# Starting VectorE's background work one k-pass earlier, with shorter pauses, and moving one conditioning step ahead of a weight split

## The chip, the cores and the metric

The kernel runs on one core of one Trainium2 chip. The metric is the device time of one execution in microseconds (us); times of before and after are medians of several executions on the same kind of chip. A core has a matrix engine (TensorE, PE in the profile, with its weight loads as PEld), VectorE (DVE), ScalarE (ACT), GpSimd (POOL) and SyncE (SP). SP issues most of the transfers from main memory; POOL and ACT issue a few of their own. Each engine works through its own list of instructions in the order in which the program wrote them, so an instruction that waits holds up everything behind it on that engine.

## The reference, cut to what matters

One layer of a decoder for 256 tokens of width 2048, batch 1:

```python
mod = (silu(c) @ w_cond + b_cond).reshape(B, 3, 3, 2048)
u = x * (1 + mod[:, 0, 1]) + mod[:, 0, 0]
h = (silu(u @ w1) * (u @ w3)) @ w2                    # SwiGLU, hidden width 5632
x = layer_norm(ALPHA * x + 0.5 * (1 + mod[:, 0, 2]) * h)
...                                                   # mixer, modulated by mod[:, 1]:
proj = u @ w_in                                       # q, k, v and s
h = concat([diff_attention(q, k, v), s5_branch(s)], -1) @ w_out
x = layer_norm(ALPHA * x + (1 + mod[:, 1, 2]) * h)
...                                                   # second SwiGLU, modulated by mod[:, 2]
```

The S5 branch is a diagonal complex state-space model with 64 groups and 64 states. Its step matrices and decay tables depend on parameters alone, so they can be prepared at any time before the mixer needs them. The same holds for `mod`, which depends on `c` alone.

## The kernel before, in words

**Jobs.** The heavy work is a list of jobs. A job takes one 128x1024 piece of fp32 weights. SP loads it (`raw`), ScalarE casts it to a reduced format (`hi`, L690), VectorE subtracts to get what the cast lost (`lo`, in `pay`, L697), and TensorE multiplies with `hi` and `lo` against activations that are split into two parts in the same way (`Uh`/`Ul`, later `Hh`/`Hl` and so on). `Stream.run` (L703) writes the jobs in order: the hooks of a job, its matmuls, the split of the piece that comes `AHEAD` = 4 jobs later (2 in the first four jobs), then the background hooks `bg`, then `drain`. There are four buffers of `raw`, of `hi` and of `lo`. Nearly all VectorE and TensorE instructions pass a helper that adds up a cost estimate of each engine, so they have line 105 in the profile and are told apart by their tiles.

**The first feed-forward.** Its first 96 jobs (4 * `NT1`) are four k-outer passes of 24 jobs, each over four of the sixteen 128-row slices of the input. A pass can only start once its quarter of the input is modulated by `mod`. Sums that must be kept between passes lie in tiles `kosum`; in the later passes VectorE adds to them. 168 further jobs finish the hidden activations and do the down projection. The last four jobs do token half 0 first, then (in `last_block`) run its residual and layer norm on VectorE and ScalarE while TensorE does token half 1; then the first transposes of the mixer follow (`turn`).

**Conditioning.** `mod` is a matrix-vector product done by VectorE: `gv_step` (L230) multiplies one 128x1024 half row block of `w_cond` by silu(c) and accumulates along the row (tiles `early` for a whole 128x2048 block that counts as two steps, `gv` for a half). There are 288 steps. Sixteen of them complete one quarter of one modulation; `finish` (L256) then forms scale and shift of two or four slices and `modulate` queues the ScalarE work for them, which `pay_mod` and `pay_late` write out (ScalarE `uf` and `Uh`, VectorE `Ul`). Until step 64 the steps are tied to job numbers (`ahead`, L1534). Each step also asks SP for later rows of `w_cond` (`gv_load`).

**Background work.** After job 96 the rest of conditioning and the preparation of the S5 branch fill VectorE's gaps. `drain` (L360), called after every job, hands out work while VectorE's estimate is below that of TensorE plus `lim`. A credit of `gv_max` steps per job limits conditioning; the rising target `gv_due` says when conditioning has precedence over the S5 list `bg5`. The S5 list is `fill` (some 110 small operations on a tile `cells`), then `rest`: for each of four quarters a load, VectorE products, ScalarE copies, transposes on TensorE and stores, and at the end two halves of decay tables (`tables`, L595; tiles `tabc` and `tabr`, stored to `scrB` by POOL). Between them stand pauses, `wait(n)`; a pause ends when TensorE's estimate has moved on by n * `S5_WAIT`. What is left of the list three jobs before the end of the first feed-forward is written out at once by `drain_s5` (L380).

**The start.** Conditioning steps 0 to 7 give the first two input slices, steps 8 to 15 the next two. Jobs 0 to 3 use the first two slices, jobs 4 to 7 the next two. Steps 8 and 9 are tied to job 0, 10 and 11 to job 1, 12 and 13 to job 2, 14 and 15 to job 3; in each job the split of a weight piece stands ahead of the steps.

## Time and profile before

| what | value |
|---|---|
| median of 3 runs | 1934.16 us (1934.05 to 1934.27) |
| the profiled execution | 1936.67 us, of which the span from the first to the last instruction is 1934.9 us |
| mean granted TensorE clock | 0.982 of full |
| TensorE busy | 1861.1 us, 96% of the span |
| VectorE busy | 1490.3 us, 77% |
| ScalarE busy | 889.4 us, 46% |
| moved by DMA | 532.36 MB, 275 GB/s on average |

The table is read from the top of the profile's page. TensorE is the busiest by far, so what counts is the time in which it stands still, and the engine that it then waits for. The other engines' idle time costs nothing by itself. Timeline rows in the quoted fences give start and duration in us, engine, line, operation, the tile written, an arrow, the tiles read with shapes, and in brackets the idle time before the instruction and what ended it. Rows of a stretch ("stages") give start:end, length, then busy time with the count of instructions in parentheses for each engine shown, then the granted clock, the DMA share and GB/s.

### The profile page before, as it was taken

How to read it: one execution, taken by the hardware profiler on the slowest of the kernel's cores; microseconds unless marked ns; L12 is line 12 of the kernel's file. 1: busy time of each engine (PE TensorE's matmuls, PEld its weight loads, DVE VectorE, ACT ScalarE, POOL GpSimd, SP SyncE). 2: the span in 40 equal slices, each digit the busy share in tenths (PEclk: the TensorE clock that was granted, in tenths of full speed). 3: DMA queues.
4: the chain of work that ended last, by engine and by line, in shares of the span. 5: the costliest groups of instructions: out<-in, count | busy, mean ns of one | idle time of the engine just before them, and what ended most of it. 6: DMA issues, size and time to landing. Idle time of an engine off the chain costs nothing.

```text
span 1934.9 us, 25434 instructions
## 1 busy us (share of the span) xinstructions
PE 1861.1 (96%) x9326; PEld 1571.3 (81%) x9326; DVE 1490.3 (77%) x2255; ACT 889.4 (46%) x1211; POOL 64.0 (3%) x119
## 2 busy tenths in 40 slices
PE   5999999999999999589999998999999999999996
PEld 4888888888888887489998886888888888888885
DVE  5889878987887899887988997887875545454568
ACT  3554444445445543343447634544444444334442
POOL 0000000000000000202120000000000000000000
PEclk9999999999999999799999998999999999999998
DMA  8998857989999997698988885998888555565563
GB/s 329 374 346 311 300 177 246 318 279 357 313 339 346 319 349 272 215 349 272 310 272 297 288 321 199 332 355 292 286 281 270 190 187 185 196 216 186 192 231 110
DMA packets 151935, 532.36 MB, mean 275 GB/s; under 512 B 21841, under 2 KB 23297, under 8 KB 150657
## 3 DMA queue, kind: packets, MB, share of 16 engines
q1 hardware_dynamic: 137234, 495.32, 73.4%
q0 software_dynamic: 6512, 23.89, 3.6%
q10 hardware_dynamic: 8064, 11.54, 1.6%
q8 instruction: 73, 1.20, 0.2%
q14 instruction: 52, 0.43, 0.1%
HBM read 513.34 MB, written 17.33 MB: 274 GB/s over the span
## 4 chain that ended last, share of the span: by engine, by line
PE 83%; DMA 5%; DVE 5%; issue 5%; ACT 1%; POOL 0%; SPq 0%; ACTq 0%; DVEq 0%; POOLq 0%
PE ps L105 83%; DMA raw<-in_f1w_dram 2%; DMA early<-in_w_cond_dram 1%; DVE lo L105 1%; DVE Y L105 1%; DVE gv L105 1%; DVE early L105 1%; ACT hi L690 0%; DMA U<-sD 0%; DMA sD<-sT 0%; DVE tabc L105 0%; DMA s5e<-scrA 0%; DMA scrB<-tabr 0%; DMA raw<-in_f2w_dram 0%; ACT Y L861 0%
## 5 line engine op out<-in xcount | busy, mean ns | idle before, releaser
L105 DVE TENSOR_TENSOR lo<-raw,hi 128x1024 fp32r<-128x1024 f32 x630 | 766.5, 1222 | 351.7 <-ACT hi L690 343.3
L690 ACT CAST hi<-raw 128x1024 fp32r<-128x1024 f32 x630 | 661.5, 1053 | 702.5 <-PE ps L105 523.6
L105 PE MATMUL ps<-hi,Uh 128*128 128x512 f32 x1472 | 583.1, 396 | 19.3 <-ACT Uh L317 15.6
L105 PE MATMUL ps<-hi,Ul 128*128 128x512 f32 x1472 | 576.8, 392 | 0.0
L105 PE MATMUL ps<-lo,Uh 128*128 128x512 f32 x1472 | 456.5, 391 | 1.4 <-DVE lo L105 1.4
L105 PEld LDWEIGHTS ps<-hi,Uh 128*128 128x128 f32 x1472 | 278.3, 189 | 80.2 <-ACT Uh L317 16.5
L105 PEld LDWEIGHTS ps<-lo,Uh 128*128 128x128 f32 x1472 | 277.9, 189 | 61.1 <-DVE lo L105 2.6
L105 PEld LDWEIGHTS ps<-hi,Ul 128*128 128x128 f32 x1472 | 278.4, 189 | 56.6 <-DVE Ul L105 0.9
L105 DVE SCALAR_TENSOR_TENSOR gv<-gv,sc 128x1024 f32<-128x1024 f32 x258 | 314.1, 1218 | 2.3 <-DMA gv<-in_w_cond_dram 1.9
L105 PE MATMUL ps<-hi,Hh 128*128 128x512 f32 (+1 forms) x716 | 274.5, 385 | 0.0
L105 PE MATMUL ps<-hi,Hl 128*128 128x512 f32 (+1 forms) x716 | 273.6, 383 | 0.0
L105 PE MATMUL ps<-lo,Hh 128*128 128x512 f32 (+1 forms) x716 | 216.6, 384 | 3.5 <-DVE lo L105 3.5
L105 PEld LDWEIGHTS ps<-lo,Hh 128*128 128x128 f32 x716 | 133.0, 188 | 30.7 <-DVE lo L105 4.3
L105 PEld LDWEIGHTS ps<-hi,Hh 128*128 128x128 f32 x716 | 134.5, 188 | 26.6 <-issue 0.4
L105 PEld LDWEIGHTS ps<-hi,Hl 128*128 128x128 f32 x716 | 134.6, 188 | 26.1
L105 PE MATMUL ps<-Uh,hi 128*128 128x256 f32 x384 | 99.8, 296 | 2.4 <-ACT sT L1143 1.9
L105 PE MATMUL ps<-Ul,hi 128*128 128x256 f32 x384 | 97.4, 290 | 0.0
L105 PEld LDWEIGHTS ps<-Uh,hi 128*128 128x128 f32 x384 | 75.8, 197 | 6.5 <-ACT sT L1143 2.7
L105 PEld LDWEIGHTS ps<-Ul,hi 128*128 128x128 f32 x384 | 75.6, 197 | 0.6 <-DVE Ul L105 0.3
L1006 ACT CAST Hh<-ps 128x512 fp32r<-128x512 f32 x44 | 25.9, 588 | 75.0 <-PE ps L105 74.9
L105 DVE TENSOR_TENSOR Hl<-ps,Hh 128x512 fp32r<-128x512 f32 x44 | 30.3, 688 | 35.5 <-ACT Hh L1006 35.5
L105 PE MATMUL ps<-Uh,lo 128*128 128x256 f32 x384 | 53.9, 283 | 0.0
(229 smaller groups left out, 1398.4 us busy)
## 6 DMA issues: line engine op xcount, KB each, us to landing
raw<-in_f1w_dram SPq DMA_DIRECT2D x264, 512.0 KB, 5.8
raw<-in_f2w_dram SPq DMA_DIRECT2D x264, 512.0 KB, 4.8
gv<-in_w_cond_dram SPq DMA_DIRECT2D x258, 512.0 KB, 6.9
raw<-in_win_a_dram SPq DMA_DIRECT2D x48, 512.0 KB, 5.2
raw<-in_wout_dram SPq DMA_DIRECT2D x32, 512.0 KB, 5.8
early<-in_w_cond_dram SPq DMA_DIRECT2D x28, 512.0 KB, 7.7
s5m<-scrB POOLq DMA_DIRECT2D x8, 1024.0 KB, 9.2
raw<-in_win_v_dram SPq DMA_DIRECT2D x16, 512.0 KB, 5.2
```

The source lines that it names most:

```text
L105: return f(*a, **k)
L690: S.copy(hi, raw)
L1006: S.copy(hh, p)
```

## The change

Five edits. First, `drain` gets its limits at job `BG_AT` = 70 instead of 96, so that conditioning and the S5 list's `fill` may run in the last k-outer pass; `rest` still joins the list at job 96. The target `gv_due` starts at job 70 and has the same end (step 160 at job 256). Second, the limit of the first feed-forward goes from 2.6 to 3.0 and its credit from 0.62 to 0.57 steps per job. Third, the pauses: `S5_WAIT` goes from 2.0 to 1.7 and the pause between the two halves of the tables from 8.0 to 4.0. Fourth, steps 14 and 15 go from job 3 to job 2, and in job 2 the steps stand ahead of the split of the fifth weight piece. Fifth, the second weight piece is split ahead of the first modulation rather than behind it.

```diff
-LIM = (2.6, 100.0, 100.0, 100.0)
-GVM = (0.62, 0.65, 0.85, 0.4)
+LIM = (3.0, 100.0, 100.0, 100.0)
+GVM = (0.57, 0.65, 0.85, 0.4)
-S5_WAIT = 2.0
+S5_WAIT = 1.7
+BG_AT = 70
...
-            rest += [(0.0, tables(0)), wait(8.0), (0.0, tables(1))]
+            rest += [(0.0, tables(0)), wait(4.0), (0.0, tables(1))]
...
                     if not j.hold:
-                        self.split_to(self.done + st["split"])
+                        if self.done != 3:
+                            self.split_to(self.done + st["split"])
                         for f in j.bg:
                             f()
+                        if self.done == 3:
+                            self.split_to(self.done + st["split"])
                         drain()
...
+        stream.split_to(2)
         pay_mod()
-        stream.split_to(2, False)
         pay_late()
-        stream.pay()
...
-            n = (8 + 2 * i + 2 if i < 4 else NS + math.ceil((i - 3) * NS / (GA[0] - 3)) if i <= GA[0] else
+            n = ((10, 12, 16, 16)[i] if i < 4 else NS + math.ceil((i - 3) * NS / (GA[0] - 3)) if i <= GA[0] else
...
-        stream.run(4 * NT1)
+        stream.run(BG_AT)
         bg5.extend(fill)
-        bg5.extend(rest)
-        new_stats()
-
         n0 = stream.done
         st["gv_due"] = lambda n: 64 + 96.0 * (n - n0) / (GV_END - n0)
         st["lim"], st["gv_max"] = LIM[0], GVM[0]
+        stream.run(4 * NT1 - BG_AT)
+        bg5.extend(rest)
+        new_stats()
```

## The prediction, made before the run

> **What bounds the kernel now.** I read the head of the page first, then what TensorE waited for, then the timeline at each long wait.

> ```profile
> PE 1861.1 (96%) x9326; PEld 1571.3 (81%) x9326; DVE 1490.3 (77%) x2255; ACT 889.4 (46%) x1211; POOL 64.0 (3%) x119
> ...
> PE ps L105 <- ACT Y L861: 18.3, 1, 18.3
> PE ps L105 <- ACT Uh L317: 15.6, 2, 7.8
> PE ps L105 <- DVE Y L105: 6.3, 2, 3.3
> PE ps L105 <- DVE lo L105: 4.9, 3, 2.2
> ```

> TensorE is the bound; of its 1934.9 - 1861.1 = 73.8 us at rest, two items stand out: one wait of 18.3 us for the normalised `Y`, and two of 7.8 us for the modulated input `Uh`, one of them before the first job, which the change leaves. The first item is the end of the first feed-forward:

> ```profile
> 771.15 1.28 DVE L105 SCALAR_TENSOR_TENSOR Y<-X,Y 128x512 f32<-128x512 f32 x2
> 772.35 3.48 DVE L105 TENSOR_TENSOR lo<-raw,hi 128x1024 fp32r<-128x1024 f32 x3
> 775.75 0.41 DVE L105 TENSOR_TENSOR tabc<-tabc,tabr 128x256 f32<-128x256 f32 x1
> ...
> 783.12 0.07 DVE L105 MEMSET tabc<- 128x16 f32 x1 [3.23 <-DMA scrB<-tabc]
> 784.80 0.07 DVE L105 MEMSET tabc<- 128x16 f32 x1 [1.61 <-DMA scrB<-tabc]
> 786.24 0.69 DVE L105 COPY tabr<-cells 128x1024 f32<-128x1024 f32 x1 [1.36 <-DMA scrB<-tabr]
> ...
> 796.34 0.68 DVE L105 TENSOR_TENSOR r<-ps,G 128x512 f32<-128x512 f32 x1
> ...
> 782.46 0.40 PE L105 MATMUL ps<-lo,Hh 128*128 128x256 f32 x2
> 801.11 1.12 PE L105 MATMUL ps<-ident,Y 128*128 128x128 f32 x4 [18.25 <-ACT Y L861]
> ...
> 807.16 0.58 PE L105 MATMUL ps<-Uh,hi 128*128 128x256 f32 x1 [0.56 <-DVE Uh L105]
> ```

> The name ACT hides the cause. From 775.75 to 796.34 VectorE works through what was left of the S5 list: the last steps of the first table half, a wait of 3.23 + 1.61 + 1.36 = 6.2 us until that half is stored, then the whole second half. The residual `r` of the last block stands behind it, and the layer norm and the transposes behind that. The same place at the mixer's end, where no list is left, shows the clean case:

> ```profile
> 1171.88 0.40 PE L105 MATMUL ps<-lo,Ah 128*128 128x256 f32 x2
> 1172.12 0.60 PE L105 MATMUL ps<-ident,Y 128*128 128x128 f32 x4
> 1175.78 1.12 PE L105 MATMUL ps<-ident,Y 128*128 128x128 f32 x4 [3.06 <-DVE Y L105]
> 1177.45 0.80 PE L105 MATMUL ps<-hi,Uh 128*128 128x512 f32 x1 [0.56 <-DVE Uh L105]
> ```

> There the first token half is normalised under the matmuls of the second, and only a 3.06 us wait for the second half remains.

> **The tail of the first feed-forward.** From the last tail matmuls to the first of the next stage it takes 807.16 - 782.46 = 24.7 us here and 1177.45 - 1171.88 = 5.6 us there. If the list is empty in time, 24.7 - 5.6 = 19.1 us go. What is late next is the second half's `Y`, which I leave in the sum.

> Is the list empty in time? What has to move is 796.34 - 775.75 = 20.6 us of VectorE time, 14.4 without the waits for the store.

> ```profile
> 226.00:297.00 71.00, 52.60 (x65) 1.00 0.55 189
> 297.00:450.00 153.00, 136.02 (x289) 1.00 0.85 291
> 450.00:691.00 241.00, 195.93 (x290) 1.00 0.94 337
> 691.00:771.00 80.00, 77.28 (x144) 1.00 0.88 313
> ...
> 300.00:381.00 81.00, 19.20 (x113) 1.00 0.86 296
> ...
> L105 DVE SCALAR_TENSOR_TENSOR gv<-gv,sc 128x1024 f32<-128x1024 f32 x13 | 15.8, 1218 | 0.0
> ```

> The first four rows are VectorE's busy time by stretch, the fifth that of the operations on `cells`, nearly all of them `fill`, the sixth the conditioning steps from 691 to 771. The last pass (226 to 297) leaves 71 - 52.6 = 18.4 us free and holds no background work. From job 70 on the target asks for 96 / 186 = 0.516 steps per job, so 26 jobs take 13.4 steps of 1.218 us, 16.3 us, and some 2 us remain for `fill`; later the steps need 0.6 - 0.516 = 0.084 fewer per job, which over 165 jobs frees 16.9 us for the list. So whichever goes first, about 18 us of work move out of the later stretch. Then the pauses: their weights in the list add up to 73, at 2.0 this is 146 us of TensorE's estimate, and 69 at 1.7 is 117, 29 us less. They bind, since from 450 to 691 VectorE is idle for 241 - 195.9 = 45 us while the list is unfinished; from 691 on it has 2.7 us in 80 and the list crawls. Ending some 29 us of pauses and 18 us of work sooner covers 20.6 us, and the tables then run where there is idle time. I take the list as done. What hides it is VectorE's idle time under TensorE; if that cover is short, the price is the remaining VectorE time, one for one.

> The waits added: none by name, but shorter pauses can let VectorE, ScalarE or TensorE meet data not yet there. After the copies of a batch the pause ends after 6.8 us rather than 8, with the next weight split four jobs ahead; I cost it at nothing; the bounds are 0 and 2.2 us, the one late `lo` row of before. The higher limit lets VectorE run 0.4 us further ahead. The three `lo` at 772.35 came late by 2.2 us, behind residual work that the change keeps; it may go (-2.2) or grow by the 0.4. I take 0, as that work is unchanged.

> **The start.** Steps 12 to 15 wait behind the fifth piece's `lo`, which waits for its transfer:

> ```profile
> 30.44 2.28 DVE L105 SCALAR_TENSOR_TENSOR early<-early,sc 128x2048 f32<-128x2048 f32 x1
> 35.71 1.23 DVE L105 TENSOR_TENSOR lo<-raw,hi 128x1024 fp32r<-128x1024 f32 x1 [2.98 <-ACT hi L690]
> 36.85 1.22 DVE L105 SCALAR_TENSOR_TENSOR gv<-gv,sc 128x1024 f32<-128x1024 f32 x1
> ...
> 39.14 1.22 DVE L105 TENSOR_TENSOR lo<-raw,hi 128x1024 fp32r<-128x1024 f32 x1
> ...
> 43.15 0.16 DVE L105 TENSOR_TENSOR bt<-bt,cst 128x2 f32<-128x2 f32 x1
> 44.41 0.43 DVE L105 TENSOR_TENSOR Ul<-uf,Uh 128x256 fp32r<-128x256 f32 x1 [1.10 <-ACT Uh L317]
> ...
> 35.93 1.05 ACT L690 CAST hi<-raw 128x1024 fp32r<-128x1024 f32 x1 [0.25 <-DMA raw<-in_f1w_dram]
> ...
> 35.97 0.61 PE L105 MATMUL ps<-lo,Uh 128*128 128x512 f32 x2
> 44.43 0.80 PE L105 MATMUL ps<-hi,Uh 128*128 128x512 f32 x1 [7.84 <-ACT Uh L317]
> 45.02 0.67 PE L105 MATMUL ps<-hi,Ul 128*128 128x512 f32 x1
> ```

> Now step 12 follows the 30.44 row at 32.7 instead of 36.85 (4.15 sooner), and the `lo` of 39.14 no longer stands among the steps (1.14 sooner, the distance to the row behind it): scale and shift are ready at 43.31 - 5.3 = 38.0, and the first matmul of job 4 can start at 39.1. But both `lo` now follow and `Ul` follows them: 38.0 + 2 x 1.14 = 40.3, so the second matmul starts at about 40.8 against 44.9 (44.41 + 0.43). The gain is 4.1 us. The rows of `w_cond` for steps 12 to 15 were asked for ahead of the fifth piece, which had landed before its `lo` at 35.71, so they are there. On SP's queue the loads for steps 16 to 23 and an input quarter, nine loads of 512 KB, now stand ahead of the ninth and tenth pieces. They also go out earlier:

> ```profile
> 36.00:40.00 4.00, 0.59 (x3) 0.16 (x1) 4.00 (x6) 0.98 (x1) 0.00 (x0) 1.00 0.34 123
> 46.00:48.00 2.00, 2.00 (x6) 1.61 (x6) 0.00 (x0) 0.48 (x1) 0.00 (x0) 0.50 0.98 344
> 48.00:50.00 2.00, 2.00 (x9) 1.55 (x9) 0.00 (x0) 0.63 (x3) 0.00 (x0) 0.85 0.95 356
> ...
> 1174.00:1176.00 2.00, 0.22 (x1) 0.23 (x2) 1.74 (x8) 0.49 (x2) 0.00 (x0) 0.74 0.00 0
> 1176.00:1184.00 8.00, 6.04 (x15) 4.09 (x15) 4.51 (x10) 2.75 (x6) 0.00 (x0) 0.50 0.18 62
> ```

> The transfer engines stood at 0.34 from 36 to 40, waiting for step 12 to free its buffer; that gap closes. At 344 GB/s a load takes 1.5 us, so the ninth piece, tenth in that order, lands by 36 + 15.2 = 51.2; job 8 starts about 40.8 + 4 x 2.73 = 51.7 or later (71 us for the 26 jobs of the stretch 226 to 297, 2.73 each). So it is near its limit: between 0 and 4.1 us may be lost, I take none, as the piece still comes first. The second piece's earlier split fills ScalarE's and VectorE's wait for the first conditioning; 0, at most 1.2 either way.

> **The clock.** After the gap that begins at 36.6 (35.97 + 0.61) the granted clock is 0.50, and by the 0.85 of the row behind it stays there until about 48.6: 4.2 us at half speed from 44.43 on, a loss of 2.1; after the 3.06 us gap at the mixer's end it is 0.74, then 0.50 with 6.04 us of TensorE work in it, 3.0 us of loss. [...]

> **Sum.** 19.1 + 4.1 = 23.2 us off the profiled execution's 1936.67 us (span 1934.9, 1.8 around it), 1913.5. That execution is 2.5 us over the median, 1934.16; off the median it is 1911.0, my forecast.

> **Rivals.**
> - *A rest of the list is still drained* (say the second half's operations, 10.1 us from 786.24 to 796.34, without the wait for the store): 1921. For it: VectorE is 97% busy from 691 to 771. Against: the 45 us of idle time before. Chance 0.12.
> - *The clock stays up* in both shorter gaps: 3.0 + 2.1 us more, 1906. [...] Against: the 1174 row. Chance 0.12.
> - *The start gives nothing*, since the ninth piece comes late: 1915. For it: ten loads. Chance 0.06.
> - *The change doesn't do what it says*: the list is bound by something other than pauses and free time, the drain stays, only the start gains: 1930. Against: 18.4 us free in a pass that had no background. Chance 0.04.
> - *Slower*: the lower credit. Step 160 must be done before the mixer's first modulation; what lacks is made up on the path at 1.218 us each. From 691 to 771 only 13 steps were done in 80 us, 0.44 per job of 2.73 us, and 0.57 with lost credits may sink that low over the whole stretch. From 20 steps short on it eats the 23.2 us; 24 short gives 1940. Against: 191 jobs x 0.57 = 108.9 steps may be taken, 96 are needed. Chance 0.04.

> **How the numbers follow.** The forecast, 1908 to 1916 around 1911.0, has 0.62. The range takes the best bounds, 23.2 + 5.1 (clock) + 2.2 (`lo`) = 30.5 off, 1904, and at the other end the drained second half, 1921. A measurement can tell some 0.2%, 3.9 us, from no change. Faster by more: 0.62 + 0.12 + 0.12 + 0.06 = 0.92; the same 0.04; slower 0.04.

> **What would show it.** Right: no `tabc` row on VectorE within 30 us of the first feed-forward's end, TensorE's transposes directly behind the last tail matmuls, `gv` rows between 226 and 297, the restart of job 4 near 39 with its second matmul near 41. Wrong: `tab` rows behind the last `lo`; waits on `lo` or `raw` between 50 and 130 us or in the last pass; a row of `gv` steps just ahead of the mixer's first `Uh`.

## The result, and the profile after

| | before | after |
|---|---|---|
| median, four executions each | 1934.11 us | 1915.44 us |
| profiled execution (span) | 1936.67 us (1934.9) | 1912.22 us (1910.4) |
| ratio after/before | | 0.9903, 95% interval 0.9881 to 0.9926 |

After is faster by 14 to 23 us. One of its four executions (2084.23 us at a granted clock of 0.846) was disturbed and is left out of the ratio; the others took 1912.22, 1914.07 and 1916.82 us. The forecast was 1911.0, with a range of 1904 to 1921.

What TensorE waited for in after, from its list of waits (total, times, longest, in us):

```profile
PE ps L106 <- ACT Uh L318: 9.7, 2, 7.6
PE ps L106 <- DVE Y L106: 6.3, 2, 3.2
...
PE ps L106 <- DVE lo L106: 3.6, 4, 1.3
PE ps L106 <- DVE kosum L106: 3.3, 3, 1.2
...
PE ps L106 <- DMA U<-sD: 2.3, 1, 2.3
```

The 18.3 us for `Y` on ScalarE are gone, the second wait for `Uh` has shrunk from 7.8 to 2.1, and a new name stands there: `kosum`. (All lines of the helper are now L106.)

The end of the first feed-forward in after, and when its table operations ran (first and last start):

```profile
773.97 0.72 PE L106 MATMUL ps<-lo,Hh 128*128 128x512 f32 x2 [1.20 <-DVE lo L106]
...
783.05 0.60 PE L106 MATMUL ps<-ident,Y 128*128 128x128 f32 x4
786.71 1.11 PE L106 MATMUL ps<-ident,Y 128*128 128x128 f32 x4 [3.06 <-DVE Y L106]
788.40 0.58 PE L106 MATMUL ps<-Uh,hi 128*128 128x256 f32 x1 [0.58 <-DVE Uh L106]
```

```profile
L106 DVE TENSOR_TENSOR tabc<-tabc,tabr x24: 180/255/693, 619.4 to 688.9; 128x16 f32<-128x16 f32 x4, 128x32 f32<-128x32 f32 x4, 128x64 f32<-128x64 f32 x4, 128x128 f32<-128x128 f32 x4
```

The list is done 85 us before the late `lo`, and the transposes stand directly behind the last matmuls. In before the same `lo` was late too:

```profile
773.62 0.73 PE L105 MATMUL ps<-lo,Hh 128*128 128x512 f32 x2 [2.20 <-DVE lo L105]
```

From the late `lo` to the mixer's first matmul it is 788.40 - 773.97 = 14.43 us, against 807.16 - 773.62 = 33.54 before: 19.1 us less.

But at that late `lo` after is 0.35 us behind before, although its start was quicker. The timeline of the start in after:

```profile
32.41 1.22 DVE L106 SCALAR_TENSOR_TENSOR gv<-gv,sc 128x1024 f32<-128x1024 f32 x1
...
37.69 2.36 DVE L106 TENSOR_TENSOR lo<-raw,hi 128x1024 fp32r<-128x1024 f32 x2
...
38.86 0.74 PE L106 MATMUL ps<-hi,Uh 128*128 128x512 f32 x1 [2.09 <-ACT Uh L318]
39.96 0.76 DVE L106 TENSOR_TENSOR Ul<-uf,Uh 128x256 fp32r<-128x256 f32 x2
40.44 0.79 PE L106 MATMUL ps<-hi,Ul 128*128 128x512 f32 x1 [0.84 <-DVE Ul L106]
```

The second matmul of job 4 starts at 40.44 instead of 45.02. The gain goes in the last pass; VectorE and TensorE there:

```profile
252.29 1.22 DVE L106 SCALAR_TENSOR_TENSOR gv<-gv,sc 128x1024 f32<-128x1024 f32 x1
...
253.43 0.19 DVE L106 SCALAR_TENSOR_TENSOR cells<-cells 128x32 f32<-128x32 f32 x1
253.54 1.28 DVE L106 TENSOR_TENSOR kosum<-ps,kosum 128x512 f32<-128x512 f32 x2
254.28 0.51 PE L106 MATMUL ps<-hi,Uh 128*128 128x512 f32 x1 [1.18 <-DVE kosum L106]
```

A sum is complete in a pair of `ps` buffers, but the addition that empties the pair stands behind a conditioning step and an operation of `fill`; TensorE needs the pair for the next sum and waits 1.18 us for it. This happens three times, 3.3 us.

To see where time goes in many runs I cut each trace at four points: the first matmul of job 0, the end of ScalarE's last copy into `kosum`, the mixer's first matmul and the second feed-forward's first matmul. The rows of before and, in the second fence, of after that the prediction does not hold:

```profile
22.94 0.80 PE L105 MATMUL ps<-hi,Uh 128*128 128x512 f32 x1 [7.80 <-ACT Uh L317]
115.19 1.07 ACT L954 COPY kosum<-ps 128x512 f32<-128x512 f32 x2
```

```profile
22.75 0.79 PE L106 MATMUL ps<-hi,Uh 128*128 128x512 f32 x1 [7.59 <-ACT Uh L318]
111.29 1.07 ACT L958 COPY kosum<-ps 128x512 f32<-128x512 f32 x2
1152.88 0.80 PE L106 MATMUL ps<-hi,Uh 128*128 128x512 f32 x1 [0.79 <-DVE Uh L106]
```

So stage I is 115.19 + 1.07 - 22.94 = 93.3 us before and 89.6 after, II (to the mixer) 690.9 and 676.0, III (the mixer) 370.3 and 364.5. What follows takes 757.5 in both. The 5.8 us of the mixer were in no term of the prediction.

### The profile page after: what moved, and what is told of

Read it like the earlier page. It is cut to its first block, busy times and chain, and to the rows that moved or that the text cites. A ratio compares the mean times of both kernels' runs of the same rounds, so it can differ in the third digit from the quotient of the medians.

```text
span 1910.4 us, 25429 instructions
## 1 busy us (share of the span) xinstructions
PE 1858.5 (97%) x9326; PEld 1567.5 (82%) x9326; DVE 1488.1 (78%) x2255; ACT 889.4 (47%) x1211; POOL 65.0 (3%) x119
## 4 chain that ended last, share of the span: by engine, by line
PE 87%; DVE 6%; DMA 4%; ACT 2%; issue 1%; POOL 0%; SPq 0%; DVEq 0%; ACTq 0%; POOLq 0%
PE ps L106 87%; DVE lo L106 2%; DVE Y L106 2%; DMA raw<-in_f1w_dram 1%; DVE gv L106 1%; ACT hi L691 1%; DMA early<-in_w_cond_dram 1%; DMA raw<-in_wout_dram 0%; DMA U<-sD 0%; DVE st L106 0%; DVE r L106 0%; DMA sD<-sT 0%; DMA early<-in_wc_dram 0%; ACT Y L865 0%; DVE early L106 0%
## 5 line engine op out<-in xcount | busy, mean ns | idle before, releaser
L106 DVE TENSOR_TENSOR lo<-raw,hi 128x1024 fp32r<-128x1024 f32 x630 | 766.3, 1222 | 342.1 <-ACT hi L691 338.5
L106 PE MATMUL ps<-hi,Uh 128*128 128x512 f32 x1472 | 583.7, 397 | 16.7 <-ACT Uh L318 9.7
L106 PE MATMUL ps<-hi,Ul 128*128 128x512 f32 x1472 | 577.5, 392 | 0.8 <-DVE Ul L106 0.8
L106 PE MATMUL ps<-lo,Uh 128*128 128x512 f32 x1472 | 457.4, 392 | 1.3 <-DVE lo L106 1.3
L106 PEld LDWEIGHTS ps<-hi,Uh 128*128 128x128 f32 x1472 | 278.7, 189 | 77.8 <-ACT Uh L318 10.4
L106 PEld LDWEIGHTS ps<-lo,Uh 128*128 128x128 f32 x1472 | 278.4, 189 | 60.9 <-DVE lo L106 2.0
L106 PEld LDWEIGHTS ps<-hi,Ul 128*128 128x128 f32 x1472 | 279.0, 190 | 58.1 <-DVE Ul L106 1.9
L106 DVE SCALAR_TENSOR_TENSOR gv<-gv,sc 128x1024 f32<-128x1024 f32 x258 | 314.2, 1219 | 1.4 <-DMA gv<-in_w_cond_dram 1.3
L106 PE MATMUL ps<-hi,Hh 128*128 128x512 f32 (+1 forms) x716 | 274.6, 385 | 0.0
L106 PE MATMUL ps<-hi,Hl 128*128 128x512 f32 (+1 forms) x716 | 273.6, 383 | 0.0
L106 PE MATMUL ps<-lo,Hh 128*128 128x512 f32 (+1 forms) x716 | 216.5, 384 | 1.8 <-DVE lo L106 1.8
L106 PEld LDWEIGHTS ps<-lo,Hh 128*128 128x128 f32 x716 | 133.0, 188 | 29.1 <-DVE lo L106 2.6
L106 PEld LDWEIGHTS ps<-hi,Hh 128*128 128x128 f32 x716 | 134.5, 188 | 26.8 <-issue 0.4
L106 PEld LDWEIGHTS ps<-hi,Hl 128*128 128x128 f32 x716 | 134.6, 188 | 26.0
L106 PE MATMUL ps<-Uh,hi 128*128 128x256 f32 x384 | 97.9, 292 | 2.4 <-ACT sT L1147 1.8
L106 PE MATMUL ps<-Ul,hi 128*128 128x256 f32 x384 | 95.7, 286 | 0.1
L106 PEld LDWEIGHTS ps<-Uh,hi 128*128 128x128 f32 x384 | 74.2, 193 | 6.2 <-ACT sT L1147 2.7
L106 PEld LDWEIGHTS ps<-Ul,hi 128*128 128x128 f32 x384 | 74.2, 193 | 0.8 <-DVE Ul L106 0.7
L106 PE MATMUL ps<-Uh,lo 128*128 128x256 f32 x384 | 53.9, 283 | 0.0
L106 DVE TENSOR_TENSOR Hl<-ps,Hh 128x512 fp32r<-128x512 f32 x44 | 30.3, 688 | 30.0 <-ACT Hh L1010 29.7
```

What stands on the lines that cost most here:

```text
L106: return f(*a, **k)
```

## Experiments

The stages in us of every trace, and the timings; each ratio is against runs of before on the same chip, whose medians there were 1935 to 1938 us.

| kernel | I | II | III | median | ratio (95%) |
|---|---|---|---|---|---|
| before, first trace | 93.3 | 690.9 | 370.3 | | |
| before_again | 92.1 | 691.5 | 369.5 | | |
| store_act | 93.5 | 690.5 | 367.7 | 1933.41 | 0.9986 (0.9977 to 0.9996) |
| start_only | 90.2 | 691.0 | 366.3 | 1934.15 | 0.9991 (0.9975 to 1.0007) |
| pauses_only | 88.7 | 675.6 | 380.0 | 1930.57 | 0.9968 (0.9956 to 0.9980) |
| pauses_credit | 90.2 | 683.9 | 370.4 | 1925.95 | 0.9951 (0.9933 to 0.9968) |
| early_only | 91.8 | 678.6 | 366.7 | 1919.49 | 0.9907 (0.9893 to 0.9922) |
| background_only | 93.9 | 674.8 | 368.1 | 1916.50 | 0.9899 (0.9881 to 0.9917) |
| old_pauses | 90.0 | 680.6 | 362.8 | 1915.99 | 0.9904 (0.9883 to 0.9925) |
| after, first trace | 89.6 | 676.0 | 364.5 | | 0.9903 (0.9881 to 0.9926) |
| after_again | 90.8 | 675.2 | 368.0 | 1914.63 | 0.9890 (0.9865 to 0.9914) |
| behind_sums | 92.1 | 674.5 | 366.8 | 1914.32 | 0.9885 (0.9865 to 0.9906) |
| ul_behind | 91.5 | 677.8 | 363.0 | 1917.94 | 0.9907 (0.9891 to 0.9922) |
| quiet_tail | 90.7 | 677.5 | 367.6 | 1914.69 | 0.9881 (0.9864 to 0.9899) |

### The start alone, and the background alone

`start_only` is before with the fourth and fifth edit of the change; `background_only` is after without them.

> Only the start is changed (conditioning steps 12 to 15 ahead of the fifth piece's split, second piece split ahead of the first modulation); all background settings are those of before. Theory: the second matmul of job 4 comes 4.6 us earlier, as in the trace of after, the lead is kept to the end of the first feed-forward, and the drain of the list stays: some 1930 us (1928 to 1931). Rival: the weight transfers set the pace between 50 and 130 us (their share is 0.93 to 0.98 there in after), so the lead is given back by job 24: 1933 to 1934.

> Only the background is changed (begun at job 70, limits, shorter pauses); the start is that of before. Theory: the wait for the normalised Y of 18.3 us goes (19.1 us), and the three waits for kosum of 1.1 to 1.2 us in the last pass are there, 3.9 us with what lies around them, and about 1 us more is lost behind them: 1919 us (1917 to 1922). Rival: the kosum waits belong to the earlier start, which lets TensorE run into weights and sums that VectorE has not finished: then there are none here and the time is 1915.

`background_only` is 19.6 us below before by its ratio (16.1 to 23.1), some 4 more than the theory's 15; about 2 of these are the mixer's in its trace (368.1 us against 370.3 and 369.5). It has the three kosum waits (1.17, 1.08, 1.08), so they do not need the early start: that rival falls.

The timing of `start_only` is inconclusive: the interval of its ratio runs from 4.8 us below before to 1.4 above, which holds 4.1 and nothing. The traces say more, and that the start gives less than it seems to at job 4. From the first matmul to job 4's second it takes 41.97 - 24.18 = 17.8 us in `start_only`, as in after (17.7), and 22.1 in before. By the end of stage I the five runs with the old start stand at 93.3, 92.1, 93.5, 93.9 and 91.8, mean 92.9; the eight with the new one (without `ul_behind`) have a mean of 90.3. So 4.4 becomes 2.6: the theory kept all of it, the rival none. From job 4's second matmul to the end of stage I the five take 70.8 us on the mean, the eight 72.6. Of these 1.8 us, 0.4 are waits for weights: three of the eight wait for `hi` at 54 to 56 us (0.66, 0.84 and, in `behind_sums`, 1.70 us), no run with the old start does. Another 0.4 is lost to half clock, which covers more of the work behind an earlier restart (2.3 us lost against 1.9). This is an estimate that counts half of TensorE's time at a granted clock of 0.50 as lost: behind job 4's second matmul that time is 5.34 us in after (40.44 to 45.78) and 3.56 in before (45.02 to 48.58), and in after matmuls on 128x512 start 0.43 us apart in it (43.16 and 43.59) and 0.23 apart behind it (48.52 and 48.75). The last 0.9 or so lies in TensorE's busy time, and its cause stays open.

### The last pass or the pauses?

`pauses_only` is after with this edit:

```diff
-BG_AT = 70
+BG_AT = 96
```

> As after, but the background begins at job 96 instead of 70, so the last pass holds none; target and pauses as in after. Theory: the shorter pauses alone (29 us of TensorE time) empty the list before the end of the first feed-forward, with its tables later than the 619 to 689 us of after but ahead of 770; the kosum waits go, 3.9 us: 1911 us. Rival: the 17 us of VectorE work done in the last pass are needed; the list is drained again in part, with tabc rows behind the last lo: 1921 to 1930.

The theory was right on the list and wrong on the time. The tables end at 745.7, nothing is drained, stage II has the full gain (675.6). But the mixer takes 380.0 us. The mixer's head on VectorE, and two waits of TensorE:

```profile
811.80 1.23 DVE L106 SCALAR_TENSOR_TENSOR gv<-gv,sc 128x1024 f32<-128x1024 f32 x1 [4.36 <-DMA gv<-in_w_cond_dram]
...
814.35 1.23 DVE L106 SCALAR_TENSOR_TENSOR gv<-gv,sc 128x1024 f32<-128x1024 f32 x1 [1.32 <-DMA gv<-in_w_cond_dram]
```

```profile
822.96 0.58 PE L106 MATMUL ps<-Uh,hi 128*128 128x256 f32 x1 [9.56 <-ACT hi L691]
...
842.31 0.58 PE L106 MATMUL ps<-Uh,hi 128*128 128x256 f32 x1 [4.94 <-ACT sT L1147]
```

Conditioning is late. The steps of `gv` in VectorE's groups up to the end of the first feed-forward, for before, after and `pauses_only`:

```profile
L105 DVE SCALAR_TENSOR_TENSOR gv<-gv,sc 128x1024 f32<-128x1024 f32 x128 | 155.7, 1218 | 0.1
```

```profile
L106 DVE SCALAR_TENSOR_TENSOR gv<-gv,sc 128x1024 f32<-128x1024 f32 x129 | 157.0, 1219 | 0.1
```

```profile
L106 DVE SCALAR_TENSOR_TENSOR gv<-gv,sc 128x1024 f32<-128x1024 f32 x121 | 147.3, 1219 | 0.1
```

Eight steps are missing against after, since 165 jobs at 0.57 allow 94. They are made up ahead of the mixer's modulation, and there they also wait for the transfers of their rows of `w_cond`: TensorE loses 14.5 us in the two waits for eight steps of 1.22. The mechanism of the prediction's slower rival is real, and dearer for each step (1.8 us) than its price; even so this run is 6 us faster than before. In after the last pass keeps it off.

`pauses_credit` has one more edit:

```diff
-GVM = (0.57, 0.65, 0.85, 0.4)
+GVM = (0.62, 0.65, 0.85, 0.4)
```

> As after, but the background begins at job 96 and the credit of conditioning is 0.62 steps per job as before, not 0.57. Theory: the run without the last pass's work lost its gain ahead of the mixer because 165 jobs x 0.57 = 94 steps are fewer than the 96 needed (149 were done at the end of the first feed-forward, where after has 157); with 0.62, 102 may be taken, so some 156 are done as in before, the two waits of 9.6 and 4.9 us in the mixer go, the list ends ahead of 771 as it did with 0.57, and nothing waits for kosum: 3 to 5 us below after. Rival: 7 more steps of 1.22 us in the first feed-forward, 8.5 us of VectorE, push the tables past its end: a drain of up to 10 us at the boundary, 5 us above after or more.

The rival was right. With 0.62 the steps are in time (128 of `gv`, as in before), and the list is not: its table operations, and the transposes behind the last matmuls:

```profile
L106 DVE TENSOR_TENSOR tabc<-tabc,tabr x24: 179/256/693, 688.2 to 785.5; 128x16 f32<-128x16 f32 x4, 128x32 f32<-128x32 f32 x4, 128x64 f32<-128x64 f32 x4, 128x128 f32<-128x128 f32 x4
```

```profile
790.84 1.12 PE L106 MATMUL ps<-ident,Y 128*128 128x128 f32 x4 [5.34 <-ACT Y L865]
```

So without the last pass one of the two was short in each run: with the short pauses the steps at 0.57 and the list at 0.62, with the pauses of before the list. The next two ask the other way round: the last pass with the old pauses (`old_pauses`: after with `S5_WAIT` 2.0 and 8.0 between the tables), and the last pass alone on the kernel before (`early_only`):

```diff
+BG_AT = 70
...
-        stream.run(4 * NT1)
+        stream.run(BG_AT)
         bg5.extend(fill)
-        bg5.extend(rest)
-        new_stats()
...
+        stream.run(4 * NT1 - BG_AT)
+        bg5.extend(rest)
+        new_stats()
```

> As after with the background begun at job 70, but with the pauses of before (2.0 and 8.0). Theory: the pauses add some 29 us of TensorE time, so the tables end near 720 to 735 us instead of 689, still ahead of 771: no drain, the same time as after within 2 us. Rival: pauses and last pass are both needed, as in the last stretch VectorE has no idle time left: tabc rows behind 771 and a drain of 5 to 20 us at the boundary.

> The kernel before with one part of the change alone: background from job 70 instead of 96 (target from there too); limit 2.6, credit 0.62, pauses of 2.0 and 8.0 and the start stay as before. Theory: the free time of the last pass is what empties the list: no tabc row behind the last lo, no wait of 18 us for Y; the kosum waits of 1.1 us are there, and as in old_pauses some waits for lo and Y of 1 to 3 us remain in the tail: from the last copy of a kosum by ScalarE to the mixer's first matmul 678 to 684 us (before: 690.9 and 691.5; old_pauses 680.6; after 676.0 and 675.3), 1920 us (1917 to 1924). Rival: with the credit of 0.62 conditioning takes the place in the last pass and the list is still drained in part, as in pauses_credit: tabc rows behind 775, Y waited for 5 us or more, 685 us or more in that stretch.

Both theories held, though in `old_pauses` the tables end at 707.9, sooner than the 720 to 735 expected. In `early_only` limit, credit, pauses and start are those of before, and still, in the same two views:

```profile
L106 DVE TENSOR_TENSOR tabc<-tabc,tabr x24: 181/256/684, 629.5 to 705.2; 128x16 f32<-128x16 f32 x4, 128x32 f32<-128x32 f32 x4, 128x64 f32<-128x64 f32 x4, 128x128 f32<-128x128 f32 x4
```

```profile
793.21 0.66 PE L106 MATMUL ps<-ident,Y 128*128 128x128 f32 x4 [3.44 <-DVE Y L106]
```

Stage II falls to 678.6, 12.6 of the 15.6 us by which the two traces of after lie below those of before. `old_pauses` differs from after in the pauses alone. Its stage II is some 5 us longer (680.6 against 676.0 and 675.2), with waits of 1.81 for `Hl`, 2.33 for `lo` and 3.44 for `Y` near its end. But its mixer is the shortest of all (362.8), and its median is only 1.4 us above that of `after_again`, within the intervals: that the shorter pauses make the whole faster is not shown. The limit of 3.0, the credit of 0.57 and the fifth edit were not run alone; `early_only` shows that the list is done without them.

### How much belongs to the change

> The changed kernel as it is, once more, beside the others on this chip. Theory: the 24.5 us between the two profiled executions hold 5.8 us of the mixer that are partly an accident of these two executions (a wait of 3.0 us for the scan's input with a fall of the clock behind it in before, of 2.3 us without one in after), so this median lies 18 to 21 us below that of before. Rival: the 5.8 us belong to the change, and this median lies 23 to 25 us below.

> The kernel before, for a second trace. Theory: the wait of 18.3 us at the end of the first feed-forward and the one of 7.8 us at job 4 stand there unchanged; the length of the mixer, 370.3 us from its first matmul to that of the second feed-forward in the first trace, varies with the wait for the scan's input and the clock behind it and comes out 2 to 5 us shorter when that wait is below 2.4 us. Rival: the mixer's 370 us are the same to 1 us, so what after gained there is the change's.

`after_again` came out 1935.05 x (1 - 0.9890) = 21.3 us below, 16.6 to 26.1 by its interval: just above the theory's 21 and below the rival's 23 to 25, which the interval does not exclude. `before_again` repeats the waits (18.25 for `Y`, 8.16 for `Uh`), but its mixer took 369.5 us with a wait of only 1.61 for the scan's input: that part of the theory fell, and the first half of its rival held. The second half does not follow, as the mixer of `after_again` took 368.0.

The granted clock tells more. In the mixer TensorE is idle for 9.6 us in before and 8.9 in after, but the time that the half clock costs there, by the same estimate half the length of its falls, is 9.4 us in before and 3.0 in after. Two falls of the clock stand in the midst of the mixer of before and not in that of after: one of 6.83 us at the wait for the scan's input, and one of 3.41 behind a second wait, for `s5e`. The first comes and goes in one and the same kernel (`after_again` has it, from 850.48 to 857.30). For the second, here are GpSimd in before, the matmul behind it, and TensorE's work at half clock that follows:

```profile
948.03 0.53 POOL L300 DMA_DIRECT2D growD<-grow  x1 [14.75 <-DVE grow L105]
948.55 0.56 POOL L1190 DMA_DIRECT2D s5e<-scrA  x1
```

```profile
954.86 2.18 PE L105 MATMUL ps<-U,s5e 128*128 128x64 f32 x16 [1.10 <-DMA s5e<-scrA]
```

```profile
956.52:959.94 3.42, 3.42 (x18) 0.50 1.02 325
```

Waiting and half clock together cost 1.1 + 1.7 = 2.8 us.

The store of a finished conditioning unit waits on GpSimd's list for VectorE, and the load of the next S5 batch waits behind it. In after conditioning is a step further on (129 against 128, above; 129 or more in every trace with the last pass's work), and the same pair comes earlier, 130.7 us after the mixer's first matmul instead of 140.9:

```profile
919.13 0.54 POOL L301 DMA_DIRECT2D growD<-grow  x1 [8.24 <-DVE grow L106]
919.66 0.57 POOL L1194 DMA_DIRECT2D s5e<-scrA  x1
```

This was tested by moving the store, and nothing else, in before:

```diff
-                GP.dma_start(growD[sub:sub + 1, i * 1024:(i + 1) * 1024].rearrange("o (a b) -> (o a) b", b=128), g)
+                S.dma_start(growD[sub:sub + 1, i * 1024:(i + 1) * 1024].rearrange("o (a b) -> (o a) b", b=128), g)
```

> The kernel before, with one transfer issued by another engine: the store of grow (end of a conditioning unit for the G scale) goes out on ScalarE's list and not on GpSimd's. Theory: in before GpSimd stands behind that store, which waits 14.8 us for VectorE's grow, and asks for the next S5 batch (s5e from scrA) only behind it at 948.6 us; that is the mixer's wait of 1.1 to 1.8 us with half the clock for some 3 us behind it. Here the wait goes, and the mixer from its first matmul to that of the second feed-forward takes 366 to 367 us instead of 369.5 to 370.3: 2 to 3 us below before. Rival: the batch is late for another reason (the tile it is loaded into comes free late, or the transfer itself), the wait of 1 us or more stays and so does the mixer's length.

The theory held in the main: the load goes out at 932.88, the wait and the fall behind it are gone, stage III is 367.7 (0.7 above the forecast), and the time falls by 0.8 to 4.5 us. The four traces with that wait (before, `before_again`, `start_only`, `pauses_credit`) have a mean stage III of 369.1, the nine without it and without late steps 366.1. The two groups overlap: `start_only`, with a wait of 1.29 us and no fall behind it, took 366.3. So about 3 us of the 5.8 belong to the change, as a side effect of conditioning being ahead, and the rest to the two executions.

### Can the last pass's price be had back?

`behind_sums` is after with this edit:

```diff
-                        drain()
+                        if j.post or not BG_AT <= self.done < 4 * NT1:
+                            drain()
```

> As after, but in jobs 70 to 95 background work is handed out only after a job that ends a sum, so that it stands behind the addition to kosum and not ahead of it. Theory: the kosum waits go while most of the last pass's work stays: 1911 to 1912 us. Rival: what is held back only moves and makes something else late (lo of the next piece or the sum after), so the time stays at 1914 to 1915.

The kosum waits of the last pass are gone, although 7.3 of the 12.2 us of steps still stand in that pass: so the order made them, as far as a run that changes order and amount together can tell. Stage II gains only about 1 us, since `lo` is late twice further on (1.20 at 741.00, 2.32 at 775.75), the second time behind a step and the end of a conditioning unit:

```profile
764.69 1.22 DVE L106 SCALAR_TENSOR_TENSOR gv<-gv,sc 128x1024 f32<-128x1024 f32 x1
...
767.04 0.16 DVE L106 SCALAR_TENSOR_TENSOR gs<-acc 128x4 f32<-128x4 f32 x1
```

The time is that of after within the interval; the rival is nearer. Two tries to mend the tail start from `behind_sums`. First `ul_behind`, then `quiet_tail`:

```diff
-GVM = (0.57, 0.65, 0.85, 0.4)
+GVM = (0.62, 0.65, 0.85, 0.4)
...
-GV_END = 256
+GV_END = 244
...
-                        if self.done != 3:
+                        if self.done not in (3, 4):
                             self.split_to(self.done + st["split"])
                         for f in j.bg:
                             f()
-                        if self.done == 3:
+                        if self.done == 4:
+                            pay_late()
+                        if self.done in (3, 4):
                             self.split_to(self.done + st["split"])
```

```diff
-GVM = (0.57, 0.65, 0.85, 0.4)
+GVM = (0.60, 0.65, 0.85, 0.4)
...
-        stream.run(len(parts[0]) - 4 * NT1 - QUIET)
+        stream.run(len(parts[0]) - 4 * NT1 - 7)
         drain_s5()
         st["lim"] = None
-        stream.run(QUIET)
+        stream.run(7)
```

> As the run behind_sums (background of the last pass only behind the sums), with three more edits: the split of the sixth piece behind the modulation of the first quarter's second half, so that Ul stands ahead of that piece's lo; credit 0.62; target step 160 at job 244 instead of 256, so that the conditioning unit does not end beside the residual work of the last matmuls. Theory: the second matmul of job 4 comes 1.2 us sooner after the first matmul of all (16.5 us instead of 17.7); the lo waits of 1.2 and 2.3 us that behind_sums had at 741 and 776 us go; from the last copy of a kosum by ScalarE (115.74 there) to the mixer's first matmul 671 to 672 us instead of 674.5 (after: 676.0 and 675.3): 1909 to 1911 us. Rival: the steps that come sooner take the S5 list's place, its tables end later than the 706 us of behind_sums, and VectorE is again late for lo in the tail: 674 to 678 us in that stretch, 1914 us or more.

> As behind_sums, but no background in the last seven jobs of the first feed-forward (three before), with credit 0.60 to keep the steps in time. Theory: the lo wait of 2.3 us at 775.75 in behind_sums came from a step and the end of a conditioning unit beside the residual work; it goes or falls below 1 us, and from the last copy of a kosum by ScalarE to the mixer's first matmul it takes 672 to 673 us instead of 674.5; the time is 1910 to 1913 us. Rival: the residual work alone makes lo late there, as in before (2.2 us) where no such end stood beside it; the stretch stays at 674 us or more, and the three steps not done are made up in the mixer.

Both missed. In `ul_behind` the steps took the list's place, its last `tabc` row starts at 778.5, and stage II is 677.8. At the start, `Ul` no longer holds up the second matmul, and the weights take the gain back (TensorE):

```profile
39.61 0.67 PE L106 MATMUL ps<-hi,Uh 128*128 128x512 f32 x1 [2.03 <-ACT Uh L318]
55.24 0.51 PE L106 MATMUL ps<-hi,Uh 128*128 128x512 f32 x1 [2.72 <-ACT hi L691]
```

In `quiet_tail` the late `lo` shrinks to 1.11, but TensorE waits 1.31 for `Hh` and 2.02 for `Hl` near 725, behind that its matmuls with `hi` on 128x512 take 0.63 us each from 728.44 to 733.13 against 0.39 at 723.17, and stage II is 677.5. Its ratio is the lowest of all and not distinguishable from that of after. No run beats after beyond the intervals.

## Why the prediction was right, point by point

- **The tail of the first feed-forward: right.** 19.1 us were forecast and 19.1 came, by the working given: the same 3.06 us for the second half of `Y` is what remains. The two sources were not equal, though. Some 18 us of VectorE's work did move into the last pass (steps 12.2, their accumulator reads 0.8, `cells` 5.1); that part alone empties the list. The 29 us of pauses alone do not: at either credit, list or conditioning is short. Nor do the two add up as in "18 us of work and 29 us of pauses sooner": the last `tabc` row starts at 795.7 in before and at 705.2 in `early_only`, 90 us sooner for the last pass's work alone. That fits the prediction's reading that the list crawls from 691 on, a stretch which it now mostly misses; no run tests this by itself.
- **The last pass and shorter pauses at nothing: the step that was mis-sized.** I costed the work in the last pass by VectorE's free time in 71 us and looked only at `lo` for an effect. It cost 3.3 us in waits for `kosum`, and 0.9 in three short waits for `s5w` and `sg` stand behind it. Stage II of the two first traces adds up as 19.1 + 1.0 (the late `lo` fell from 2.20 to 1.20) - 3.3 - 0.9 = 15.9 against 14.9 measured; the last 1.0 I cannot assign.
- **The start: right in place, too large in effect.** 4.1 us were forecast at job 4 and 4.4 came from the first matmul on (4.6 from the span's start); the order 12 to 15, `lo`, `lo`, `Ul` is as worked out. About 2.6 remain at the end of stage I. That the weights might come late was the rival "the start gives nothing"; it holds in part, in some executions, for 0.4 of the 1.8 us.
- **The clock: right.** It fell at the start (38.95 to 45.78) and at the mixer's head (786.47 to 793.30) in after too, so the rival "the clock stays up" was wrong. The falls in the midst of the mixer were in no term.
- **Left out: the mixer.** About 3 us came from conditioning being a step ahead there, through GpSimd's list. The prediction ended at the mixer's first matmul; the change's effect did not.
- **The sum.** 23.2 forecast; 2.6 + 15.6 + 3.0 = 21.2 by the stages, 18.8 and 21.3 by the two timings. The miss of the last pass and of the start was partly covered by the gain in the mixer, so that the time is nearer than the terms is in part luck.
- **The rivals.** "A rest of the list is still drained" and "slower through the credit" did not happen here, yet each happened in a neighbouring run, `pauses_credit` and `pauses_only`. For the slower one 1.22 us a step was too cheap: in `pauses_only` 8 missing steps cost 14.5 us, since a late step also waits for its transfer. At that price some 13 missing steps, not 20, would eat the forecast 23.2 us (an estimate from this one run).

## What to carry to other kernels

Free time of an engine, summed over a stage, says how much background work fits, not where: here an operation of 1.22 us ahead of the one that frees a buffer cost TensorE 1.08 to 1.18 us each time, and behind it nothing at that place. When a list of background work is not done in time, give it an earlier start before shortening its pauses, and follow what else is then ahead: every engine list in which something waits for that work (here a store on GpSimd with a load behind it) moves with it. Compare traces by stages cut at the same events: stage II repeats to 1 us here, where the times of before on one chip spread over 14 (1928.55 to 1942.98).

## What the runs showed of the hardware

In before and after all changes of the granted clock, from 30 us after the start to 20 us before the end, lie on one grid of 3.41 us to within 0.01 us (in before 41.75, 48.58, 867.78 and 874.61 are four of them; the outer two are 832.86 us, 244 periods, apart). From the span's start an edge lies at 41.75 in before and at 38.95 in after, 2.80 us apart and so not on the same grid. Windows of after on its grid (start:end, length, TensorE busy, granted clock, DMA share, GB/s):

```profile
35.54:38.95 3.41, 1.32 (x7) 1.00 1.03 405
38.95:42.37 3.42, 2.58 (x6) 0.50 1.02 410
42.37:45.78 3.41, 3.41 (x10) 0.50 1.04 413
45.78:49.19 3.41, 3.41 (x16) 1.00 1.02 407
```

```profile
844.51:847.92 3.41, 2.06 (x18) 1.00 1.03 262
847.92:851.33 3.41, 2.46 (x22) 1.00 1.03 408
```

The first window is idle for 2.09 us, and the clock falls at its end. The wait of 2.30 us for the scan's input lies across an edge, 1.35 and 0.95 us, and the clock stays. The second trace of before has a wait of only 1.61 us, all in one window and with matmuls of 64 columns behind it, and falls:

```profile
864.60:868.02 3.42, 1.81 (x16) 1.00 1.03 339
868.02:871.43 3.41, 3.41 (x18) 0.50 1.03 414
```
